# Hybrid decoder trunk in fp32: the low-rank rows and the rotary key are turned through HBM scratch and VectorE instead of TensorE, small projections three units later, last output piece 128 wide

## The chip, the cores and the metric

The kernel runs on one core of a Trainium2 chip. TensorE (PE) multiplies, VectorE (DVE) and ScalarE (ACT) compute element by element, GpSimd (POOL) does small things, SyncE (SP) issues nearly all transfers between HBM and the on-chip memory. The metric is the device time of the program in microseconds (us), as a median of several runs.

## The reference

The input is x, 256 tokens of width 1024, in float32. Two layers follow, and a final RMSNorm. One layer is a mixer of three branches with gates, and a squared-ReLU MLP:

```python
h = rms_norm(x, attn_norm[l])
p = h @ w_in
(cq, ckv, k_rope, mq, mk, mv, rq, rk, rv, rg, g_mla, g_moba, g_ret) = jnp.split(p, IN_SPLIT_IDX, axis=-1)
...
cq = rms_norm(cq, q_norm_g)            # 256 columns
ckv = rms_norm(ckv, kv_norm_g)         # 128 columns
q = (cq @ w_q_up)                      # 8 heads of 64 + 32 (rotary)
kv = (ckv @ w_kv_up)                   # 8 heads of 64 + 64
k_pe = apply_rope(k_rope, cos, sin)    # one rotary key of 32 columns for all heads
...
merged = (jax.nn.sigmoid(g_mla) * (o_mla @ w_branch_mla)
          + jax.nn.sigmoid(g_moba) * (o_moba @ w_branch_moba)
          + jax.nn.sigmoid(g_ret) * (o_ret @ w_branch_ret))
x = x + merged @ w_out
x = x + jnp.square(jax.nn.relu(rms_norm(x, mlp_norm[l]) @ w_up)) @ w_down
```

The change bears on cq, ckv and k_rope: after the projection they lie with tokens across the partitions ("rows"), and the next products want them with tokens along the free dimension, so they are turned.

## The kernel before

The 256 tokens are two tiles of 128 (t = 0, 1). Weights are streamed once, in the order that `weight_plan` writes down, as tiles `raw` of 128x1024 (four buffers). ScalarE rounds each to its high part `whi` and VectorE forms the remainder `wlo` (L211, L213, six buffers each). Each product of the reference is made of three on TensorE, high by high, high by low, low by high (`three`, L232 to L234), which share an accumulator in PSUM.

The work of a layer is a list of units (`prog`), each some twelve products on one weight tile: `start` (layer 0) or `b0` and `mq`, then `mk`, `mv`, the gates `gmla0`, `gmla1`, `gmoba0`, `rqk`, `rv`, `gmoba1`, `rg`, the branches `bmla0` and so on, `wout`, then the MLP. `at(slot(key, j), step)` hangs other work behind unit j of a key: attention scores, turns, group norm. A scheduler then settles each engine's own order from this program order. So what stands at which slot decides how much product work lies between a step and its user.

Two ways of turning a matrix are in use. One is a TensorE transpose into PSUM. The other is a round trip: `send` (L391) writes a 128x1024 tile `far` to HBM scratch with one transfer of 512 KB, `receive` (L397) reads it back as `blocks` with four transfers of 128 KB that put 32x32 blocks in their places, and `turn_into` (L405) transposes within the blocks on VectorE. SP issues all these transfers, in one line with the weights.

`c_norms` (from L571) copies the first projection to `c0`, scales cq and ckv by their norms and writes the turned rotary key `krx`. `c_turn` (L657) transposes these by eight TensorE instructions (six at L666, two at L669) into PSUM tiles `pct`, splits them with the gain into `cTh` and `cTl` (L247 on ScalarE, L248 on VectorE), and copies the rotary part through `krT` into the keys `KK` (L674 to L676). The small projections `qrope`, `qnope` and `kvup` use cTh and cTl; they are inserted before units mv0, mv1 and mv2, and the scheduler lets their products mix with those of mv. The attention steps are counted from `first`, which is the slot of unit mv3.

The end of the program is written out by hand. The last output half (columns 512 to 1023 of tile t = 1) is made in two pieces of 256 columns, by 12 products each. After the first piece VectorE adds (L1135), and multiplies by the final gain (L1171); after the last piece (`plast`) it adds (L1137), sums the squares (L1175), forms the sum `fst` (L1178). GpSimd raises it to the power -1/2 (L1183), ScalarE scales one half (L1184) and VectorE the other, and two transfers write the output.

Of the kernel before, what the change touches and what calls it, by code (L numbers as in the profile page):

```python
# [13 lines left out]
P = 128  # L14
# [44 lines left out]
def weight_plan():  # L59
# [20 lines left out]
    for l in range(L):  # L80
# [11 lines left out]
        mv, plan = plan[-4:], plan[:-4]  # L92
        for i, (key, name, kt, cols) in enumerate(
            (("qrope", "mla_w_q_up", 2, C_QROPE), ("qnope", "mla_w_q_up", 2, C_QNOPE), ("kvup", "mla_w_kv_up", 1, C_KV))
        ):
            block((l, key), name, kt, cols, kt)
            plan.append(mv[i])
        plan.append(mv[3])
        for i in range(2):
            gate("mla", i)  # L100
# [46 lines left out]
def trunk(ctx: ExitStack, tc: tile.TileContext, gx, wts, consts, gfin, gnorm, xtok, out):  # L147
# [28 lines left out]

    krx = [cp.tile([P, P], F32, name=f"krx{t}") for t in range(NT)]
    for t in range(NT):
        nc.gpsimd.memset(krx[t], 0.0)
# [56 lines left out]
    def gain(c):  # L236
        return G[:, c : c + 1]
# [326 lines left out]
    def layer(l, xn, before):  # L564

        c0 = []
# [4 lines left out]
        def c_norms():  # L571
            accs = b0
            if l:
                for n in range(KD):
                    xn.square(n)
                xn.stats()
            for t in range(NT):
                ct = w2k("c0")
                c0.append(ct)
# [8 lines left out]
                nc.vector.tensor_scalar(ct[:, 0:MLA_QR], ct[:, 0:MLA_QR], m[:, 4:5], None, op0=ALU.mult)  # L588
                kv = ct[:, MLA_QR : MLA_QR + MLA_KVR]
                nc.vector.tensor_scalar(kv, kv, m[:, 5:6], None, op0=ALU.mult)  # L590
                kr = ct[:, 384:416].rearrange("p (h two n) -> p h two n", h=1, two=2)
                rope(kr, K_COS_MLA, K_SIN_MLA, t, 16, 1, 32)
                for i in range(2):
                    dst = krx[t][:, 64 * (1 - i) : 64 * (1 - i) + 64].rearrange("p (two n) -> p two n", two=2)
                    nc.vector.tensor_copy(dst[:, :, 16 * i : 16 * i + 16], kr[:, 0, :, :])
# [61 lines left out]
        def c_turn():  # L657
# [4 lines left out]
            pts = [misc_tile("pct") for _ in range(2)]  # L662
            for k in range(3):
                pt = pts[k // 2][:, (k % 2) * S : (k % 2) * S + S]
                for t in range(NT):
                    nc.tensor.transpose(pt[:, P * t : P * t + P], c0[t][:, P * k : P * k + P], ident)  # L666
            pkr = pts[1][:, S : 2 * S]
            for t in range(NT):
                nc.tensor.transpose(pkr[:, P * t : P * t + P], krx[t], ident)  # L669
            for k in range(3):  # L670
                pt = pts[k // 2][:, (k % 2) * S : (k % 2) * S + S]
                split(pt, c["h"][:, k, :], c["l"][:, k, :], gain(G_CQ + 3 * l + k))
            krT = sb.tile([P, S], F32, name="krT", tag="xsq", bufs=2)
            nc.scalar.activation(krT, pkr, AF.Copy)  # L674
# [3 lines left out]
        at(slot("mk", 1 if l else 2), c_turn)  # L678
# [103 lines left out]
        at(first + 26, lambda: omobaT.extend((t4("omobah"), t4("omobal"))))  # L782
# [33 lines left out]
        attention(omobaT, moba_score, lambda: mqkv["mv"], MB_D**-0.5, [first + i for i in (11, 14, 17, 20)], first + 28)  # L816
# [3 lines left out]
        or_ps, aT, gn, oret = [], {}, [], []  # L820
# [36 lines left out]
        def group_norm():  # L857
# [23 lines left out]
            oret.append(both)  # L881
# [8 lines left out]
        def rg_done(accs):  # L890
            for t in range(NT):
                z, th, o = w2k("rg"), w2k("tg"), oret[0][:, :, t]
# [3 lines left out]
                nc.vector.scalar_tensor_tensor(o, o, 0.5, z.rearrange("p (g w) -> p g w", g=4), op0=ALU.mult, op1=ALU.mult)  # L896
            oret[0] = send(oret[0])
# [395 lines left out]
```

## Time and profile before

| | before |
|---|---|
| median of 3 runs | 815.45 us (815.39 to 815.56) |
| the profiled execution, device time | 814.98 us |
| its span in the profile | 812.9 us |
| PE busy | 804.9 us (99%), 3860 instructions |
| VectorE busy | 586.8 us (72%) |
| ScalarE busy | 458.3 us (56%) |
| GpSimd busy | 29.2 us (4%) |
| chain of work that ended last | PE 97% |
| mean DMA rate | 237 GB/s |

Busy time is the union of an engine's instructions; a short product's own duration in a timeline overlaps the next one's, so the step from start to start says what one costs. The chain is followed back from the last instruction to what released it.

### The profile page before, as it was taken

Reading aid. Unit: us, or ns where it says so; the run is one execution under the profiler, and the core shown is the slowest. Engines: PE = TensorE matmul, PEld = TensorE weight load, DVE = VectorE, ACT = ScalarE, POOL = GpSimd, SP = SyncE. Lnnn points to the kernel's source line nnn. Section 1 sums busy time; section 2 is a strip of 40 time slices with the busy share of each in tenths; the row PEclk is TensorE's granted clock in tenths of the full one; section 3 lists DMA queues with packets and bytes.
Section 4 is the critical chain, followed back from the end, with each engine's and each line's share of the span. In section 5 each row is a group of like instructions: output and inputs, shape, how many; then the busy total and the mean of one; then the engine's idle time right before and its main releaser. Section 6 shows DMA issues by size and latency. Waiting matters only on the chain.

```text
span 812.9 us, 11108 instructions
## 1 busy us (share of the span) xinstructions
PE 804.9 (99%) x3860; PEld 668.7 (82%) x3860; DVE 586.8 (72%) x1062; ACT 458.3 (56%) x714; POOL 29.2 (4%) x37
## 2 busy tenths in 40 slices
PE   9999999999999999999999999999999999999996
PEld 7888778888888888888888887788888888888885
DVE  6877897877786566666589678878778767665655
ACT  7686655555565455454577856646455555454542
POOL 0100000000040000000000000000002200000000
PEclk9999999999999999999999999999999999999999
DMA  9886989677567777777468778885675788887851
GB/s 352 293 299 195 281 267 264 191 226 231 176 212 249 221 257 259 253 239 243 152 207 249 247 236 252 298 258 182 206 236 178 238 268 273 281 273 246 258 184 52
DMA packets 75799, 192.72 MB, mean 237 GB/s; under 512 B 8416, under 2 KB 32352, under 8 KB 75744
## 3 DMA queue, kind: packets, MB, share of 16 engines
q1 hardware_dynamic: 75168, 191.16, 72.8%
q10 hardware_dynamic: 576, 0.87, 0.3%
q8 instruction: 30, 0.49, 0.2%
q14 instruction: 25, 0.20, 0.1%
HBM read 169.97 MB, written 22.02 MB: 236 GB/s over the span
## 4 chain that ended last, share of the span: by engine, by line
PE 97%; DMA 1%; issue 1%; DVE 0%; ACT 0%; SPq 0%; POOLq 0%; POOL 0%; DVEq 0%
PE acc L232 21%; PE acc L233 21%; PE acc L234 21%; PE pup L234 7%; PE pup L233 7%; PE pup L232 7%; PE acc L971 4%; PE acc L973 2%; PE po L470 1%; PE ps_s L746 1%; PE ps_s L441 1%; DMA raw<-wts 1%; PE ps_s L745 0%; PE acc L637 0%; PE acc L636 0%
## 5 line engine op out<-in xcount | busy, mean ns | idle before, releaser
L211 ACT ACTIVATE whi<-raw 128x1024 fp32r<-128x1024 f32 (+3 forms) x286 | 291.3, 1026 | 223.3 <-PE acc L234 125.2
L213 DVE TENSOR_TENSOR wlo<-raw,whi 128x1024 fp32r<-128x1024 f32 (+3 forms) x286 | 335.0, 1179 | 105.8 <-ACT whi L211 104.9
L232 PE MATMUL acc<-whi,xs 128*128 128x512 f32 (+1 forms) x384 | 151.8, 396 | 0.0
L234 PE MATMUL acc<-whi,xs 128*128 128x512 f32 (+1 forms) x384 | 149.3, 390 | 0.0
L233 PE MATMUL acc<-wlo,xs 128*128 128x512 f32 (+1 forms) x384 | 149.2, 389 | 0.0
L234 PE MATMUL pup<-whi,xs 128*128 128x512 f32 x256 | 99.8, 390 | 0.0
L233 PE MATMUL pup<-wlo,xs 128*128 128x512 f32 x256 | 99.6, 389 | 0.0
L232 PE MATMUL acc<-whi,hidden 128*128 128x512 f32 (+1 forms) x256 | 99.4, 388 | 0.0
L232 PE MATMUL pup<-whi,xs 128*128 128x512 f32 x256 | 99.3, 389 | 0.0
L233 PE MATMUL acc<-wlo,hidden 128*128 128x512 f32 (+1 forms) x256 | 99.2, 387 | 0.0
L234 PE MATMUL acc<-whi,hidden 128*128 128x512 f32 (+1 forms) x256 | 98.6, 388 | 0.0
L232 PEld LDWEIGHTS acc<-whi,xs 128*128 128x128 f32 x384 | 72.0, 188 | 16.6 <-issue 1.0
L234 PEld LDWEIGHTS acc<-whi,xs 128*128 128x128 f32 x384 | 72.1, 188 | 14.6
L233 PEld LDWEIGHTS acc<-wlo,xs 128*128 128x128 f32 x384 | 72.2, 188 | 13.8
L406 DVE STREAM_TRANSPOSE turnedup<-blocks 128x512 f32<-128x512 f32 x32 | 22.6, 708 | 55.0 <-DMA blocks<-far 55.0
L233 PEld LDWEIGHTS pup<-wlo,xs 128*128 128x128 f32 x256 | 48.0, 188 | 9.9
L234 PEld LDWEIGHTS acc<-whi,hidden 128*128 128x128 f32 x256 | 48.1, 188 | 9.8
L233 PEld LDWEIGHTS acc<-wlo,hidden 128*128 128x128 f32 x256 | 48.1, 188 | 9.8
L232 PEld LDWEIGHTS acc<-whi,hidden 128*128 128x128 f32 x256 | 48.0, 188 | 9.8
L234 PEld LDWEIGHTS pup<-whi,xs 128*128 128x128 f32 x256 | 48.1, 188 | 9.7
L232 PEld LDWEIGHTS pup<-whi,xs 128*128 128x128 f32 x256 | 48.0, 188 | 9.8
L251 ACT ACTIVATE hidden<-turnedup 128x512 fp32r<-128x512 f32 x32 | 20.3, 633 | 58.6 <-DVE turnedup L406 58.6
(234 smaller groups left out, 957.1 us busy)
## 6 DMA issues: line engine op xcount, KB each, us to landing
raw<-wts SPq DMA_DIRECT2D x264, 512.0 KB, 4.5
blocks<-far SPq DMA_DIRECT2D x104, 128.0 KB, 3.0
far<-relu SPq DMA_DIRECT2D x16, 512.0 KB, 3.8
far<-blocks SPq DMA_DIRECT2D x16, 384.0 KB, 4.2
turned<-far SPq DMA_DIRECT2D x64, 96.0 KB, 3.3
raw<-wts SPq DMA_DIRECT2D x7, 464.0 KB, 8.0
raw<-wts SPq DMA_DIRECT2D x4, 416.0 KB, 4.8
xrow<-xtok SPq DMA_DIRECT2D x4, 256.0 KB, 7.9
```

Of the source, the lines that this page charges most:

```text
L211: nc.scalar.activation(hi[:, cs], raw[:, cs], AF.Copy)
L213: nc.vector.tensor_sub(lo[:, cs], raw[:, cs], hi[:, cs].bitcast(F32))
L232: nc.tensor.matmul(o, ah, bh, start=start, stop=False)
L233: nc.tensor.matmul(o, ah, bl, start=False, stop=False)
L234: nc.tensor.matmul(o, al, bh, start=False, stop=stop)
L251: nc.scalar.activation(hi, src, AF.Copy)
L406: nc.vector.transpose(dst.rearrange("p n (a c) -> p n a c", a=4), src)
L441: nc.tensor.matmul(o, a[rows], b[rows], start=True, stop=True)
L470: nc.tensor.matmul(dst, vh, moving, start=i == 0, stop=i == 1)
L746: nc.tensor.matmul(o[:, P : 3 * P], q[:, P:S], k, start=True, stop=True)
L971: nc.tensor.matmul(acc, w[0][:, k, :], m, start=k == 0, stop=False)
L973: nc.tensor.matmul(acc[:, :S], w[1][:, k, :], mT[k // 4][:, k % 4, 0], start=False, stop=k == KD - 1)
```

## The change

- The rows and the rotary key of both tiles are written into one tile `crows` of the form that `send` takes (L587 and L595 of the kernel after), and sent at the end of `c_norms`. `receive` stands at unit mk1 in layer 0 and mq3 in layer 1. `c_turn` stands at mv0 in layer 0 and mk2 in layer 1 and does two VectorE transposes into `cturned`. The split and the key copies read from there. The 16 TensorE transposes and ScalarE's copies to krT are gone.
- `qrope` is inserted before mv3, `qnope` before gmla0 0, `kvup` before gmla0 1; the weights are in that order too. `first` is gmla0 2, three units later.
- MoBA's score pairs are at `first` + 11, 13, 16, 19 (were 11, 14, 17, 20) and its values at bmla0 1 (was `first` + 28). The retention turn, scores and values stand at gmoba1 2, rg 1 and rg 3 (were gmoba1 0, gmoba1 3 and rg 1). The multiplication by the gate rg is done in `group_norm`, which sends the result itself.
- The last output piece begins at column CUT = 896, so the two pieces are 384 and 128 wide.

```diff
+        for i in range(2):
+            gate("mla", i)
+        mv, gmla, plan = plan[-12:-8], plan[-8:], plan[:-12]
+        plan += mv[:3]
+        for (key, name, kt, cols), behind in (
+            (("qrope", "mla_w_q_up", 2, C_QROPE), mv[3:]),
+            (("qnope", "mla_w_q_up", 2, C_QNOPE), gmla[:1]),
+            (("kvup", "mla_w_kv_up", 1, C_KV), gmla[1:]),
         ):
             block((l, key), name, kt, cols, kt)
-            plan.append(mv[i])
-        plan.append(mv[3])
+            plan += behind
...
+            rows = pair_tile("crows")
+            nc.gpsimd.memset(rows[:, :, :, 96:], 0.0)
...
-                nc.vector.tensor_scalar(ct[:, 0:MLA_QR], ct[:, 0:MLA_QR], m[:, 4:5], None, op0=ALU.mult)
-                kv = ct[:, MLA_QR : MLA_QR + MLA_KVR]
-                nc.vector.tensor_scalar(kv, kv, m[:, 5:6], None, op0=ALU.mult)
+                for k in range(3):
+                    nc.vector.tensor_scalar(
+                        rows[:, :, t, 32 * k : 32 * k + 32], ct[:, P * k : P * k + P].rearrange("p (g c) -> p g c", g=4),
+                        m[:, 4 + k // 2 : 5 + k // 2], None, op0=ALU.mult,
+                    )
...
+                    c0 = 96 + 16 * i
+                    nc.vector.tensor_copy(rows[:, 2 * (1 - i) : 4 - 2 * i, t, c0 : c0 + 16], kr[:, 0, :, :])
+            c["far"] = send(rows)
...
-            pts = [misc_tile("pct") for _ in range(2)]
+            turned = sb.tile([P, 4, S], F32, name="cturned", tag="t4", bufs=T4)
+            for t in range(NT):
+                turn_into(turned.rearrange("p n (t c) -> p n t c", t=NT)[:, :, t], c["in"][t])
             for k in range(3):
-                pt = pts[k // 2][:, (k % 2) * S : (k % 2) * S + S]
-                for t in range(NT):
-                    nc.tensor.transpose(pt[:, P * t : P * t + P], c0[t][:, P * k : P * k + P], ident)
...
+                split(turned[:, k], c["h"][:, k, :], c["l"][:, k, :], gain(G_CQ + 3 * l + k))
+            krT = turned[:, 3]
             nc.vector.tensor_copy(KK[0:64, 1::2, :], krT[0:64, None, :].to_broadcast([64, 4, S]))
             nc.vector.tensor_copy(KK[64:P, 0::2, :], krT[64:P, None, :].to_broadcast([64, 4, S]))
 
-        at(slot("mk", 1 if l else 2), c_turn)
+        def c_in():
+            c["in"] = receive(c["far"])
+
+        at(slot(*(("mq", 3) if l else ("mk", 1))), c_in)
...
-        for i, unit in enumerate((qrope, qnope, kvup)):
-            prog.insert(slot("mv", i), ((unit.__name__, 0), unit))
-        at(slot("mv", 1), qr_turn)
+        at(slot(*(("mk", 2) if l else ("mv", 0))), c_turn)
...
+        for unit, behind in ((qrope, ("mv", 3)), (qnope, ("gmla0", 0)), (kvup, ("gmla0", 1))):
+            prog.insert(slot(*behind), ((unit.__name__, 0), unit))
+        at(slot("gmla0", 0), qr_turn)
...
-        first = slot("mv", 3)
+        first = slot("gmla0", 2)
...
-        attention(omobaT, moba_score, lambda: mqkv["mv"], MB_D**-0.5, [first + i for i in (11, 14, 17, 20)], first + 28)
+        attention(omobaT, moba_score, lambda: mqkv["mv"], MB_D**-0.5, [first + i for i in (11, 13, 16, 19)], slot("bmla0", 1))
...
-            oret.append(both)
+                o = both[:, :, t]
+                nc.vector.scalar_tensor_tensor(o, o, 0.5, rg[t].rearrange("p (g w) -> p g w", g=4), op0=ALU.mult, op1=ALU.mult)
+            oret.append(send(both))
...
-        at(slot("gmoba1", 0), ret_turn)
+        at(slot("gmoba1", 2), ret_turn)
         for i in range(2):
-            at(slot("gmoba1", 3), lambda i=i: ret_scores(i))
+            at(slot("rg", 1), lambda i=i: ret_scores(i))
         for h in range(RT_H):
-            at(slot("rg", 1), lambda h=h: ret_values(h))
-        at(slot("rg", 1), group_norm)
+            at(slot("rg", 3), lambda h=h: ret_values(h))
+        at(slot("rg", 3), group_norm)
...
-                    cs = slice(512 + 256 * half, 768 + 256 * half)
+                    cs = slice(CUT, D) if half else slice(512, CUT)
+                    n = cs.stop - cs.start
...
+CUT = 896
```

How the order on the engines changes is shown at the place in layer 0 where the turned rows are made and used. Lines of the kernel after are two lower from L196 on, so L230 to L232 there are the three products. On PE before, the transposes of c and krx stand among the products of mv (xs is the normed input, whi and wlo a weight tile):

```order
L234 MATMUL acc<-whi,xs_91 128x512
L666 MATMUL pct<-K,c_339 128x128 x2
L666 MATMUL pct<-K,c_358 128x128
L666 MATMUL pct<-K,c_339 128x128
L666 MATMUL pct<-K,c_358 128x128 x2
L669 MATMUL pct<-K,krx_81 128x128
L232 MATMUL acc<-whi,xs_91 128x512
```

On PE after, at the first use of the turned rows in layer 0 (qrope into misc, qnope into acc):

```order
L232 MATMUL acc<-whi,xs_90 128x512
L230 MATMUL misc<-whi,cTh 128x256
L231 MATMUL misc<-wlo,cTh 128x256
L230 MATMUL misc<-whi,cTh 128x256
L231 MATMUL misc<-wlo,cTh 128x256
L230 MATMUL acc<-cTh,whi 128x256 x2
L232 MATMUL misc<-whi,cTl 128x256
```

The transposes are gone, all 48 products of mk and all 48 of mv now stand ahead of the first product with cTh, and six products with cTh stand ahead of the first with cTl.

On VectorE before, the key copies of layer 0, with the splits cTl and rotations of mk around them:

```order
L248 SCALAR_TENSOR_TENSOR cTl<-pct,GX,cTh 128x256 x2
L366 TENSOR_TENSOR mk<-ropea,ropeb 128x4x8
L367 TENSOR_TENSOR mk<-ropea,ropeb 128x4x8
L213 TENSOR_TENSOR wlo<-raw,whi 128x1024
L364 TENSOR_TENSOR ropea<-mk,K 128x64
L365 TENSOR_TENSOR ropeb<-mk,K 128x64
L675 COPY KK<-krT 64x4x256
L676 COPY KK<-krT 64x4x256
```

On VectorE after, the same place:

```order
L211 TENSOR_TENSOR wlo<-raw,whi 128x1024
L404 STREAM_TRANSPOSE cturned<-blocks 128x4x128 x2
L211 TENSOR_TENSOR wlo<-raw,whi 128x1024
L669 COPY KK<-cturned 64x4x256
L670 COPY KK<-cturned 64x4x256
L246 SCALAR_TENSOR_TENSOR cTl<-cturned,GX,cTh 128x256 x3
L211 TENSOR_TENSOR wlo<-raw,whi 128x1024
```

The three splits cTl, which stood ahead of the key copies, now stand behind the transposes, one weight split and both key copies. On SP after, the transfers of this stretch of layer 0:

```order
L194 DMA raw<-wts 128x1024 x5
L392 DMA far<-crows 128x1024
L392 DMA far<-mq 128x1024
L194 DMA raw<-wts 128x1024
L399 DMA blocks<-far 32x4x256 x8
L392 DMA far<-mk 128x1024
```

The rows' send is new and stands ahead of mq's; their four receives are among the eight behind one weight load, where before four stood.

## Rows read from the trace of the kernel before

**Rows 1.** Busy time by stretches: stretch, us, engines' busy us, PE clock, DMA.

```profile
0.00:8.00 8.00, 6.36 (x21) 4.76 (x21) 2.56 (x6) 4.18 (x8) 0.76 (x9) 1.00 0.76 264
8.00:806.50 798.50, 798.49 (x3840) 663.98 (x3840) 582.44 (x1051) 453.43 (x706) 27.86 (x27) 1.00 0.74 238
```

**Rows 2.** Timeline of PE, layer 1: start us, us, operation, count [idle before].

```profile
433.27 0.38 PE L666 MATMUL pct<-K,c 128*128 128x128 f32 x2
...
433.72 0.60 PE L666 MATMUL pct<-K,c 128*128 128x128 f32 x4
434.15 0.38 PE L669 MATMUL pct<-K,krx 128*128 128x128 f32 x2
...
434.61 0.39 PE L234 MATMUL acc<-whi,xs 128*128 128x512 f32 x1
...
438.94 0.28 PE L232 MATMUL misc<-whi,cTh 128*128 128x256 f32 x1
```

**Rows 3.** Timeline of PE, first and last of the 24 end products.

```profile
803.51 0.28 PE L232 MATMUL acc<-whi,hidden 128*128 128x256 f32 x1
...
806.26 0.28 PE L234 MATMUL plast<-whi,hidden 128*128 128x256 f32 x1
```

**Rows 4.** Timeline of VectorE, the tail.

```profile
805.87 0.42 DVE L1171 TENSOR_TENSOR y<-xr,gf 128x256 f32<-128x256 f32 x1
806.58 0.42 DVE L1137 TENSOR_TENSOR xr<-xr,plast 128x256 f32<-128x256 f32 x1 [0.29 <-PE plast L234]
...
807.57 0.22 DVE L1178 SCALAR_TENSOR_TENSOR fst<-fst 128x1 f32<-128x1 f32 x1
```

**Rows 5.** Timeline of ScalarE, the tail.

```profile
808.46 0.72 ACT L1184 ACTIVATE y<-y,fr 128x512 f32<-128x512 f32 x1 [2.08 <-POOL fr L1183]
```

**Rows 6.** Timeline of VectorE, layer 0, around the rows and their turn.

```profile
35.35 0.28 DVE L590 TENSOR_SCALAR c<-c,ssc 128x128 f32<-128x128 f32 x1
...
36.22 1.22 DVE L213 TENSOR_TENSOR wlo<-raw,whi 128x1024 fp32r<-128x1024 f32 x1
...
37.64 0.27 DVE L595 COPY krx<-c 128x32 f32<-128x32 f32 x2
...
39.85 0.48 DVE L248 SCALAR_TENSOR_TENSOR cTl<-pct,GX,cTh 128x256 fp32r<-128x256 f32 x1 [0.78 <-ACT cTh L247]
...
46.45 0.69 DVE L676 COPY KK<-krT 64x1024 f32<-64x1024 f32 x1
...
55.56 1.30 DVE L406 STREAM_TRANSPOSE turnedqk<-blocks 128x512 f32<-128x512 f32 x2
```

**Rows 7.** Timeline of PE, layer 0, first product of mk.

```profile
25.65 0.39 PE L232 MATMUL acc<-whi,xs 128*128 128x512 f32 x1
```

**Rows 8.** Timelines of SP and VectorE: sends, receives and first transposes of round trips.

```profile
155.69 0.33 SPq L394 DMA_DIRECT2D far<-oret  x1
165.54 0.45 DVE L406 STREAM_TRANSPOSE oy<-blocks 128x256 f32<-128x256 f32 x1 [2.03 <-DMA blocks<-far]
435.91 0.42 SPq L394 DMA_DIRECT2D far<-mq  x1
442.72 1.75 SPq L401 DMA_DIRECT2D blocks<-far  x4
645.39 0.33 SPq L394 DMA_DIRECT2D far<-relu  x1
653.11 0.71 DVE L406 STREAM_TRANSPOSE turnedup<-blocks 128x512 f32<-128x512 f32 x1 [2.07 <-DMA blocks<-far]
```

**Rows 9.** Timelines of PE and VectorE, layer 0: retention's last products, low part, use.

```profile
143.51 0.39 PE L855 MATMUL por<-rv,prob 128*128 128x128 f32 x2
168.59 1.28 DVE L252 TENSOR_TENSOR oretl<-oy,oreth 128x512 fp32r<-128x512 f32 x2
179.39 0.39 PE L232 MATMUL acc<-whi,oreth 128*128 128x512 f32 x1
```

**Rows 10.** Timeline of PE, the first products of the program.

```profile
1.42 3.51 PE L546 MATMUL warm<-zero 128*128 128x512 f32 x8 [1.42 <-DVE zero L175]
```

More of the change, by code (lines that the diff above doesn't have):

```diff
@@ L91, in weight_plan @@
         block((l, "mv"), "w_in", KD, C_MV, 2)
-        mv, plan = plan[-4:], plan[:-4]
-        for i, (key, name, kt, cols) in enumerate(
-            (("qrope", "mla_w_q_up", 2, C_QROPE), ("qnope", "mla_w_q_up", 2, C_QNOPE), ("kvup", "mla_w_kv_up", 1, C_KV))
+        for i in range(2):
[6 more added lines that the diff above has]
+            (("kvup", "mla_w_kv_up", 1, C_KV), gmla[1:]),
         ):
             block((l, key), name, kt, cols, kt)
-            plan.append(mv[i])
-        plan.append(mv[3])
-        for i in range(2):
-            gate("mla", i)
+            plan += behind
         gate("moba", 0)
@@ L175, in trunk @@
     nc.vector.tensor_copy(zero, zf)
-    krx = [cp.tile([P, P], F32, name=f"krx{t}") for t in range(NT)]
-    for t in range(NT):
-        nc.gpsimd.memset(krx[t], 0.0)
     order, loaded = list(where), {}
@@ L661, in c_turn @@
             mla["v"] = [w2k("vml") for _ in range(NT)]
-            pts = [misc_tile("pct") for _ in range(2)]
+            turned = sb.tile([P, 4, S], F32, name="cturned", tag="t4", bufs=T4)
+            for t in range(NT):
+                turn_into(turned.rearrange("p n (t c) -> p n t c", t=NT)[:, :, t], c["in"][t])
             for k in range(3):
-                pt = pts[k // 2][:, (k % 2) * S : (k % 2) * S + S]
-                for t in range(NT):
-                    nc.tensor.transpose(pt[:, P * t : P * t + P], c0[t][:, P * k : P * k + P], ident)
[L667 to L674, printed above, removed]
+                split(turned[:, k], c["h"][:, k, :], c["l"][:, k, :], gain(G_CQ + 3 * l + k))
+            krT = turned[:, 3]
             nc.vector.tensor_copy(KK[0:64, 1::2, :], krT[0:64, None, :].to_broadcast([64, 4, S]))
             nc.vector.tensor_copy(KK[64:P, 0::2, :], krT[64:P, None, :].to_broadcast([64, 4, S]))
-        at(slot("mk", 1 if l else 2), c_turn)
+        def c_in():
+            c["in"] = receive(c["far"])
+        at(slot(*(("mq", 3) if l else ("mk", 1))), c_in)
         def nope(dst, w, ks, copy):
@@ L781, in layer @@
             branch(l, "bmla", half, omlaT, th_mla, merged)
-        at(first + 26, lambda: omobaT.extend((t4("omobah"), t4("omobal"))))
+        at(slot("bmla0", 0), lambda: omobaT.extend((t4("omobah"), t4("omobal"))))
         qkT = {}
@@ L895, in rg_done @@
                 nc.vector.scalar_tensor_tensor(z, th, 1.0, z, op0=ALU.add, op1=ALU.mult)
-                nc.vector.scalar_tensor_tensor(o, o, 0.5, z.rearrange("p (g w) -> p g w", g=4), op0=ALU.mult, op1=ALU.mult)
-            oret[0] = send(oret[0])
+                rg.append(z)
         def oret_in():
@@ L1172, in layer @@
                     else:
-                        add(t, cs, more[:, 0:256])
+                        add(t, cs, more[:, 0:n])
                         junk = w2k("fsq")
                         nc.vector.tensor_tensor_reduce(
-                            junk[:, 0:256], xr[:, t, cs], xr[:, t, cs], 1.0 / D, EPS, ALU.mult, ALU.add, st[:, 5:6]
+                            junk[:, 0:n], xr[:, t, cs], xr[:, t, cs], 1.0 / D, EPS, ALU.mult, ALU.add, st[:, 5:6]
                         )
```

12 lines of the change are left out of this document (4 added, 8 removed).

## The prediction

> **What bounds the kernel now.** I read the busy time by stretches first: TensorE (PE) works 798.49 of the 798.50 us between 8 and 806.5 us [rows 1]. So only three things can move the time: work taken from PE, work given to PE, and a new moment at which PE waits. VectorE, ScalarE and the DMA queues cost nothing until they are late for PE or carry the tail. After that I read the timeline of each place that the diff touches: the TensorE transposes, the last products and the tail behind them, and the stretch of layer 0 in which the low-rank rows are used. A product of 512 columns comes every 0.228 us (19 steps from 434.61 to 438.94) [rows 2], one of 256 columns every 0.1196 us (23 steps from 803.51 to 806.26) [rows 3].
>
> **Transposes taken away.** In layer 1 the eight transposes stand between 433.27 and 434.61, with two 512-wide products among them [rows 2]: 1.34 - 2 x 0.228 = 0.884 us. Layer 0 has eight of the same shape, so PE loses 2 x 0.884 = **-1.77 us**. On the other side each layer gains one send of 512 KB, four receives of 128 KB, two VectorE transposes and two scalings; VectorE and the queue have room for them on average, and what they cost depends on when their result is there (below).
>
> **Tail, last piece 128 wide.** The last 24 products took 23 steps of 0.1196, so 2.87 us with the last. Now 12 are 384 wide, which I put halfway between the two rates, 0.174, so 2.09 us; 12 are 128 wide. No product of this kind and width is in the trace. A line through the rates of 512 and 256 goes to 0.066 at 128, and a product of 128 columns should not be dearer than one of 512, 0.228: these are the ends. The nearest row is the TensorE transpose of 128 columns, four in 0.43 from 433.72 to 434.15 [rows 2], 0.108 each. I take 0.11: 1.32 us. PE then ends 2.09 + 1.32 - 2.87 = +0.54 later (ends: +0.01 and +1.96).
>
> VectorE behind it: the multiply for the first piece started at 805.87, the last addition at 806.58, 0.32 after PE's last start [rows 3, 4]. The first piece is now ready (2.09 - 12 x 0.1196 = 0.65) later, so the multiply starts at 806.52 and, 384 wide, is done at 807.08: VectorE took 0.42 for 256 columns [rows 4] and 0.28 for a 128-wide scaling [rows 6], so I put 384 at 0.56. PE's last start at 806.80 frees the last addition at 807.12. Its 128 columns take 0.28 instead of 0.42, and the reduction behind it saves the same, so the sum of squares, formed at 807.57 before, comes at 807.57 + 0.54 - 0.28 = 807.83: **+0.26**. After it ScalarE's 512-wide scaling of 0.72 [rows 5] is not changed, so VectorE's two steps beside it, of which one gets narrower and one wider, gain nothing. The ends of the 128-wide step give +0.22 (then the 384-wide multiply sets it: 807.08 for 806.58, less 0.28) to +1.7.
>
> **Layer 0, the new wait.** Before, the small projections could start as soon as eight transposes and the split were done. Now their operands go rows, HBM, receive, VectorE transposes, split, and PE meets them after the 96 products of mk and mv. PE's side: the first mk product starts at 25.65 [rows 7]; 96 x 0.228 = 21.9; PE arrives at 47.5. Six 256-wide products use only the high part (cTh), 0.72; at 48.25 it needs the low part (cTl).
>
> The operand's side: VectorE's last write of the rotary key began at 37.64 and took 0.27 [rows 6], so it ends at 37.9. Six scalings for four add some 0.4, and one weight split ahead of them is now only 512 wide, which takes about 0.55 off; I leave 37.9. How long the round trip takes I read from the kernel's other ones, from the send's issue to VectorE's first transpose: retention output 155.69 to 165.54 = 9.85; the quickest 645.39 to 653.11 = 7.7; the slowest was sent at 435.91 and its receives were issued only at 442.72 [rows 8], 6.8 later; with half of 9.85 for the way back, an estimate of 11.7. I take 9.85, since here too a send of 512 KB and weight loads share the queue: transposes start at 47.75. Two of 512 columns took 1.30 [rows 6]: 49.05. Then VectorE's order has one weight split (1.22, so about 1.15 to the next start), two copies into KK (0.69 each) and the first cTl (0.48) [rows 6]: 50.2, 51.6, 52.1. PE waits from 48.25 to 52.1: **+3.9 us**. Nothing fills it: the products behind it in PE's order all need cTh or cTl, and the next gate unit stands behind them. Others queue behind the waits: on SP the send of the rows holds mq's send and the weight load behind it until 37.9; on VectorE the transposes, and on ScalarE the high part cTh, hold the next weight splits. All these weights are for products behind the projections, and PE has the weights of mv and of all three projections by then, so I add nothing. With the quickest trip the wait is 3.9 - 2.15 = 1.75; with 11.7 it is 5.75.
>
> The Trainium skill, page "DMA: Bandwidth & Descriptors", section "Anatomy of one DMA — SWDGE (gpsimd) path", gives a transfer as 2.0 us plus its bytes / 436 KB per us; for the way out and back that is an estimate of 3.2 + 3.2 = 6.4 us, and the wait would be about 0.45. The trace disagrees: even its quickest trip takes 7.7, and the sum goes by 9.85.
>
> **Layer 1.** PE comes to the projections 96 products after the start of mk, which is 0.88 earlier than 438.94 + 48 x 0.228 = 449.9, so 449.0, and needs cTl at 449.7. The transposes on PE started at 433.27, when the rows were ready; with the send I put the full rows at about 434.6 (an estimate: the added scalings and a few rope steps behind it). 434.6 + 9.85 + 1.30 + two copies 1.38 + a split 1.15 + 0.48 = 448.8. So **0**, with 0.9 to spare; a trip of 11.7 gives +0.95.
>
> **Moved steps.** The retention values and norm, the MoBA values, and the pairs' scores issue the same instructions as before, only at other units; PE's share stays. What could be late is the retention output for its branch: from the last products (143.51) to its low part done (168.59 + 1.28) it took 26.4, and PE used it at 179.39 [rows 9], 35.9 after them. The products are now 24 steps (one unit, 5.5 us) later, which leaves 30.4: covered by 4. MoBA's output is now used 24 products after its values, 5.5 us, where the order of before had 48; the group norm that stood in VectorE's way there lost the gate's multiplies to an earlier place. I count both at **0**.
>
> **Sum**, on the profiled execution: 814.98 - 1.77 + 0.26 + 3.9 + 0 = 817.4; that execution lies 0.47 below the median, so **817.8** as the median. A difference under 0.2% (1.6 us: 813.8 to 817.1) is about what a measurement here cannot tell from none. Without any wait the sum is 813.9.
>
> **Rivals.**
> - *The wait is short.* A trip of 7.7 gives a wait of 1.75 and 815.7; each step of VectorE that goes ahead of the transposes, up to the split and the copies, takes its time off as well. For it: the two sides are only 4 us apart in a sum of six terms. Against it: the retention output's trip, of the same size and in the same layer, took 9.85 [rows 8]. By the page's figure above the time would be 814.4.
> - *No wait and a good tail: faster.* It needs the operand by 48.25, so 3.9 off the chain, and the tail at its low end: 813.5 to 813.8. Mechanism: the rows are sent two us earlier and the trip is the quickest; it decides at a wait below 0. The trace of before shows no such pair.
> - *Half rate after the wait.* The first eight 512-wide products of the program took 3.51 [rows 10], 0.44 each. If PE comes back so from a wait of 3.9, eight products cost another 1.7: 819.5. Against it: the granted clock reads 1.00 over that first stretch [rows 1], and the wait is short.
> - *A late hand-off later*, retention or MoBA output, by 2 us in each layer: 821.8. It decides when the retention chain takes over 30.4 or MoBA's over 5.5.
> - *128-wide products at 0.228*: tail +1.7 instead of +0.26: 819.3.
>
> **Chances.** The forecast (a layer-0 wait from 3.2 to 5.6, 817.1 to 819.5) 0.44; wait short 0.33; faster 0.12; the three that add to the wait together 0.11. Slower is 0.44 + 0.11 = 0.55, within 0.2% 0.33, faster 0.12. The range, 813.9 to 820.8, leaves out the faster case and about half of the last three; the forecast's own range is 817.1 to 819.5.
>
> **What would show it.** Right: no transposes on PE before the projections, one gap on PE of 3 to 5 us near 48 to 52 released by VectorE's cTl, none near 449, last product about 0.5 later after the tail's start. Wrong: no gap in layer 0 (then the trip or the rows were earlier than I read), a gap in layer 1, gaps at the retention or MoBA branch, or 128-wide steps far from 0.11.

## The result and the profile after

The changed kernel takes **824.86 us** (median of six runs, 821.61 to 826.58) where the kernel before takes 815.42 (814.64 to 816.02) on the same chip: a ratio of 1.0110, interval 1.0088 to 1.0131. It is slower, as was the likeliest case, but by 9.4 us and not by 2.4, and the time lies outside the range of 813.9 to 820.8. The profiled execution took 824.47 with a span of 822.2, 9.5 more than that of before.

Where TensorE (PE) waited is read from its view of waits. Columns: who waited for whom, us in total, how often, the longest.

```profile
PE misc L230 <- ACT cTh L245: 3.5, 1, 3.5
...
PE ps_r L439 <- DVE turnedrqk L404: 1.2, 1, 1.2
PE por L852 <- DVE prob L845: 1.2, 1, 1.2
PE misc L232 <- DVE cTl L246: 0.9, 2, 0.7
```

Before, PE was busy for 798.49 of 798.50 us after its start [rows 1]; now four waits stand there. The first is the forecast one, at the turned rows; the last is the rest of it, with 0.2 in layer 1. The two between are new: the retention scores (ps_r) wait for their turned queries and keys, and the values (por) for prob, which VectorE makes from those scores.

The timeline of PE at the first wait (start, us, operation, idle before it):

```profile
47.06 0.39 PE L232 MATMUL acc<-whi,xs 128*128 128x512 f32 x1
50.91 0.58 PE L230 MATMUL misc<-whi,cTh 128*128 128x256 f32 x1 [3.46 <-ACT cTh L245]
51.29 0.42 PE L231 MATMUL misc<-wlo,cTh 128*128 128x256 f32 x1
...
53.30 0.58 PE L232 MATMUL misc<-whi,cTl 128*128 128x256 f32 x1 [0.73 <-DVE cTl L246]
53.68 0.41 PE L230 MATMUL misc<-whi,cTh 128*128 128x256 f32 x1
53.89 0.41 PE L231 MATMUL misc<-wlo,cTh 128*128 128x256 f32 x1
...
56.88 0.31 PE L230 MATMUL acc<-cTh,whi 128*128 128x256 f32 x1
57.02 0.28 PE L231 MATMUL acc<-cTl,whi 128*128 128x256 f32 x1
57.14 0.28 PE L232 MATMUL acc<-cTh,wlo 128*128 128x256 f32 x1
...
58.58 0.40 PE L230 MATMUL acc<-whi,xs 128*128 128x512 f32 x1
```

Two things are to be seen. PE was done with mv at 47.06 + 0.23 = 47.29 and could have used the low part six products later, at 48.0; it got it at 53.30, so the wait is **5.3 us**. And behind the wait a 256-wide product comes every 0.213 us (53.68 to 53.89) until about 56.9, and only then every 0.12 as in [rows 3]: 15 steps that cost 0.093 more each, **1.4 us**. The view by stretches shows the same as a clock (columns as in [rows 1]):

```profile
50.00:54.00 4.00, 2.35 (x9) 2.06 (x10) 3.96 (x8) 2.26 (x4) 0.00 (x0) 0.51 1.02 412
54.00:58.00 4.00, 4.00 (x25) 4.00 (x25) 2.25 (x6) 1.52 (x4) 0.00 (x0) 0.64 1.03 412
58.00:62.00 4.00, 4.00 (x22) 3.40 (x21) 3.18 (x7) 3.93 (x7) 0.00 (x0) 1.00 0.34 87
```

The granted clock is 0.51, the level of 1.2 GHz, right after the idle stretch, and 1.00 again from 58 on. The Trainium skill, page "TensorE: Matmul & The Clock Gate", section "Back-to-back issue gap", gives the step at the lower level as the columns over 1.2 GHz, by which 256 columns are an estimate of 213 ns; the trace agrees with 0.213 us.

The operand's side, from the timelines of VectorE, SP and ScalarE:

```profile
36.69 1.23 DVE L211 TENSOR_TENSOR wlo<-raw,whi 128x1024 fp32r<-128x1024 f32 x1
...
38.62 0.27 DVE L595 COPY crows<-c 128x32 f32<-128x32 f32 x2
...
49.02 1.30 DVE L404 STREAM_TRANSPOSE cturned<-blocks 128x512 f32<-128x512 f32 x2 [4.20 <-DMA blocks<-far]
50.24 1.18 DVE L211 TENSOR_TENSOR wlo<-raw,whi 128x1024 fp32r<-128x1024 f32 x1
51.35 0.68 DVE L669 COPY KK<-cturned 64x1024 f32<-64x1024 f32 x1
52.04 0.69 DVE L670 COPY KK<-cturned 64x1024 f32<-64x1024 f32 x1
52.76 1.27 DVE L246 SCALAR_TENSOR_TENSOR cTl<-cturned,GX,cTh 128x256 fp32r<-128x256 f32 x3
```

```profile
38.96 0.33 SPq L392 DMA_DIRECT2D far<-crows  x1
39.34 0.42 SPq L392 DMA_DIRECT2D far<-mq  x1
...
43.03 4.23 SPq L399 DMA_DIRECT2D blocks<-far  x8
```

The rows are ready at 38.9, are sent at 38.96, and VectorE's first transpose starts at 49.02, after 4.20 of its own idle time: a round trip of 10.06. The order of the steps behind it is the forecast one.

The transposes on PE are gone. At the end of the program PE's 128-wide products follow one another at 0.11 us (the last three start at 815.63, 815.74 and 815.86), and its last product starts 9.60 later than before [rows 3].

### The profile page after: what moved, and what is told of

It reads as the page before. It is cut to its first block, busy times and chain, and to the rows that moved or that the text cites. A ratio compares the mean times of both kernels' runs of the same rounds, so it can differ in the third digit from the quotient of the medians.

```text
span 822.2 us, 11085 instructions
## 1 busy us (share of the span) xinstructions
PE 807.9 (98%) x3844; PEld 670.4 (82%) x3844; DVE 587.5 (71%) x1070; ACT 455.9 (55%) x712; POOL 29.4 (4%) x37
## 4 chain that ended last, share of the span: by engine, by line
PE 79%; DVE 8%; DMA 6%; issue 3%; ACT 2%; SPq 1%; POOL 0%; POOLq 0%; DVEq 0%; ACTq 0%
PE acc L230 16%; PE acc L231 16%; PE acc L232 16%; PE pup L232 7%; PE pup L231 7%; PE pup L230 7%; PE acc L970 4%; DVE wlo L211 3%; DMA blocks<-far 2%; DMA raw<-wts 2%; PE acc L972 2%; PE po L468 1%; DMA far<-crows 1%; ACT whi L209 1%; DMA far<-blocks 1%
## 5 line engine op out<-in xcount | busy, mean ns | idle before, releaser
L230 PE MATMUL acc<-whi,xs 128*128 128x512 f32 (+1 forms) x384 | 151.5, 395 | 0.0
L232 PE MATMUL acc<-whi,xs 128*128 128x512 f32 (+1 forms) x384 | 148.8, 389 | 0.0
L232 PE MATMUL pup<-whi,xs 128*128 128x512 f32 x256 | 99.8, 390 | 0.0
L230 PE MATMUL acc<-whi,hidden 128*128 128x512 f32 (+1 forms) x256 | 99.6, 389 | 0.0
L230 PE MATMUL pup<-whi,xs 128*128 128x512 f32 x256 | 99.3, 389 | 0.0
L232 PE MATMUL acc<-whi,hidden 128*128 128x512 f32 (+1 forms) x256 | 98.8, 388 | 0.0
L230 PEld LDWEIGHTS acc<-whi,xs 128*128 128x128 f32 x384 | 72.0, 188 | 17.1 <-issue 2.0
L232 PEld LDWEIGHTS acc<-whi,xs 128*128 128x128 f32 x384 | 72.1, 188 | 14.8
L231 PEld LDWEIGHTS acc<-wlo,hidden 128*128 128x128 f32 x256 | 48.1, 188 | 9.9
L230 PEld LDWEIGHTS acc<-whi,hidden 128*128 128x128 f32 x256 | 48.1, 188 | 9.9
L232 PEld LDWEIGHTS pup<-whi,xs 128*128 128x128 f32 x256 | 48.1, 188 | 9.6
L232 PEld LDWEIGHTS acc<-whi,hidden 128*128 128x128 f32 x256 | 48.0, 188 | 9.7
L230 PEld LDWEIGHTS pup<-whi,xs 128*128 128x128 f32 x256 | 47.9, 188 | 9.8
```

Source lines behind the costliest of these rows:

```text
L230: nc.tensor.matmul(o, ah, bh, start=start, stop=False)
L231: nc.tensor.matmul(o, ah, bl, start=False, stop=False)
L232: nc.tensor.matmul(o, al, bh, start=False, stop=stop)
```

## The experiments

Their medians are compared with the kernel before on the same chip; edits are to the changed kernel where nothing else is said.

### Which part loses the time

**The order of after, with the TensorE transposes.** Both layers make the turned rows as before; the later projections, the moved steps and the cut at 896 stay.

```diff
+                    nc.tensor.transpose(pt[:, P * t : P * t + P], c0[t][:, P * k : P * k + P], ident)
...
-        at(slot(*(("mk", 2) if l else ("mv", 0))), c_turn)
+        at(slot("mk", 1 if l else 2), c_turn)
```

> The changed kernel, but the rows and the rotary key are turned by the eight TensorE transposes of before, at mk2 and mk1; the three-unit delay of the small projections, the moved attention and retention steps and the 384/128 tail stay. Theory A (the loss begins at the wait for the turned rows in layer 0): no gap of PE near 47 to 57 us and no half clock there; of the changed kernel's excess the 6.5 us that this stretch lost come back and 1.8 us of transposes return, so about 820. Theory B (the wait for the retention rows near 145 us and for prob near 154 us is a follow-up of the layer-0 wait): these two gaps (2.7 us) go too, so about 817. If they stay, the moved steps make them by themselves. Rival C (the three-unit delay and the moved steps cost the time, not the turn): about 824, as the changed kernel.

815.97 for 815.27, ratio 1.0007 (0.9998 to 1.0016). PE waits only at the program's start. So the moved steps, the later projections and the new cut cost some 0.7 us at most by themselves, and neither the first wait nor those at the retention appear without the turn through HBM.

**The cut alone**, on the kernel before.

```diff
-                    cs = slice(512 + 256 * half, 768 + 256 * half)
+                    cs = slice(CUT, D) if half else slice(512, CUT)
...
+CUT = 896
```

> The kernel before with only the last output piece changed to 384 and 128 columns. My sum: PE ends 0.5 later and the program 0.26 later, so 815.7, ratio 1.0003, nothing that can be told from none. If 128-wide products cost no less than their columns' share, the program ends 0.2 later; if as much as a 512-wide one, 1.7 later. Rival: the shorter last piece shortens the tail by more than PE loses, ratio below 0.9995.

815.55 for 815.27, 1.0014 (1.0000 to 1.0028): too small for the medians, so the timelines of PE and VectorE decide.

```profile
806.67 0.28 PE L233 MATMUL plast<-wlo,hidden 128*128 128x128 f32 x1
806.79 0.28 PE L234 MATMUL plast<-whi,hidden 128*128 128x128 f32 x1
```

```profile
806.53 0.56 DVE L1172 TENSOR_TENSOR y<-xr,gf 128x384 f32<-128x384 f32 x1
807.10 0.29 DVE L1137 TENSOR_TENSOR xr<-xr,plast 128x128 f32<-128x128 f32 x1
...
807.83 0.22 DVE L1179 SCALAR_TENSOR_TENSOR fst<-fst 128x1 f32<-128x1 f32 x1
```

PE's last product starts at 806.79 (forecast 806.80), the sum of squares is formed at 807.83 (forecast 807.83), where it was 807.57 [rows 4]: +0.26.

**The HBM turn in one layer only.** The other layer keeps the TensorE transposes, in the order of after.

```diff
+        if FAR[l]:
...
+            at(slot(*(("mq", 3) if l else ("mk", 1))), c_in)
+        else:
...
+            at(slot("mk", 1 if l else 2), c_turn)
...
+FAR = (False, True)
```

> The changed kernel with the turn through HBM and VectorE in layer 1 only; layer 0 turns by the TensorE transposes as before (at mk2). Theory A (layer 0 makes the loss; layer 1 hides the trip but for 0.7 to 0.9 us of waits and gives back 0.88): like the run with TensorE turns in both layers, 815.9 to 816.2. Rival (layer 1 costs its share too, since the same queues are loaded): 817 or more.

In layer 1 only: 815.93 for 815.04, 1.0012 (1.0003 to 1.0022). PE waits 0.2 for cTl in the trace, and 1.2 for prob, both in layer 1.

> The changed kernel with the turn through HBM and VectorE in layer 0 only; layer 1 by the TensorE transposes. Theory A: the whole loss, 822 to 825, as the changed kernel. Rival (loss spread over both layers): 819 to 820.

In layer 0 only (FAR = (True, False)): 824.62, 1.0114 (1.0097 to 1.0131), as much as the whole change loses. It is made up otherwise, though. PE waits 4.6 for cTh and 0.7 for cTl and gets the low part 6.4 us after it could have used it (54.51 for 48.1), the half rate behind that costs 2.3 (25 steps), and at the retention PE waits only 0.3. The clock is low until about 60:

```profile
50.00:54.00 4.00, 1.65 (x6) 1.35 (x6) 3.73 (x6) 2.26 (x4) 0.00 (x0) 0.51 1.03 370
54.00:58.00 4.00, 3.49 (x16) 3.49 (x17) 2.38 (x4) 0.31 (x2) 0.00 (x0) 0.50 0.88 359
```

**No trip through HBM.** VectorE transposes the blocks of the rows where they lie, so that the turned rows are another matrix; PE does the products of after with it.

```diff
-            c["far"] = send(rows)
+            c["rows"] = rows
...
-                turn_into(turned.rearrange("p n (t c) -> p n t c", t=NT)[:, :, t], c["in"][t])
+                turn_into(turned.rearrange("p n (t c) -> p n t c", t=NT)[:, :, t], c["rows"][:, :, t].rearrange("p g (a c) -> p g a c", c=32))
```

> The changed kernel, with the rows of both layers turned on VectorE straight from the tile in which they are made, without send and receive (the 32x32 blocks stay in their places, so the turned rows are another matrix). The whole change but for the trip. Theory A (the trip is the whole loss): no gap near 47 us, none at the retention scores, and the 1.77 us of transposes are won against the run with TensorE turns: 815.97 - 1.77 = 814.2. Rival C (a part of the loss comes from VectorE's transposes or the moved steps): above 815.5.

814.64 for 815.12, 0.9988 (0.9978 to 0.9998); PE waits only at the start. VectorE's transposes, the key copies and the splits behind them still stand in its order, so it is the trip that loses the time. The gain is 0.5, though, where 1.5 was expected. The trace says why: PE's first mk product starts at 26.15 for 25.65 [rows 7], 0.5 later; from there to the first product of the MoBA branch it saves 0.71, from that to the same place in layer 1 0.67 (instead of 0.88 each), and the tail's 0.54 on PE comes on top: its last product starts 0.35 earlier in all.

### Half rate behind the wait

**Spare work on PE.** 22 products of 512 columns, whose result nobody reads, stand ahead of mv's last unit in layer 0, so that PE is busy while the rows are under way.

```diff
+            if l == 0:
+                spare = misc_tile("spare")
+                for i in range(FILL):
+                    nc.tensor.matmul(spare, wh[:, 0, 0:P], wh, start=True, stop=True)
...
+FILL = 22
```

> The changed kernel with 22 products of 512 columns into a spare PSUM tile ahead of the last unit of mv in layer 0, from the weights of the rope projection alone; the result is not touched. They take about 5.0 us of PE in the time in which it waits. Theory A (the half clock from 50.9 to 56.9 us comes from PE's idle time before it): the granted clock stays at 1.00, the 256-wide products step by 0.12 us instead of 0.21, and PE gains about 1.3 us (33 products behind the first with cTl at 53.3 end near 57.3 instead of 58.6). Rival (the clock falls for another reason, for instance DMA traffic): clock 0.5 there as before, no gain. In both the wait for the data itself stays, covered by the added products.

821.96 for 815.27, 1.0080 (1.0067 to 1.0093).

```profile
44.45 5.15 PE L696 MATMUL spare<-whi 128*128 128x512 f32 x22
...
53.64 0.39 PE L232 MATMUL misc<-whi,cTl 128*128 128x256 f32 x1 [0.60 <-DVE cTl L246]
53.86 0.28 PE L230 MATMUL misc<-whi,cTh 128*128 128x256 f32 x1
53.98 0.28 PE L231 MATMUL misc<-wlo,cTh 128*128 128x256 f32 x1
```

The operand comes at the same time, 53.6 for 53.3, and a kernel that does 5.0 us more on PE is no slower than the changed kernel: PE had that time to spare. Behind the wait the products now come every 0.12 and the granted clock stays at 1.00. The size of this effect alone was measured with the pairs of before, since the retention waits (below) also changed here:

> The run with MoBA's pairs as before (no retention gaps), with the 22 products into a spare tile in the layer-0 wait. Theory A (the half clock behind the idle time is a cost of its own): clock 1.00 at 50 to 58 us and about 1.3 us less than the run with the pairs alone, so 819.6 beside 820.9. Rival (the first fill gained only because the retention gaps were missing in it, and the half clock costs nothing, since cTl and the weights set the pace there): no difference between the two.

> The run with MoBA's pairs as before, unaltered, on the same chip as the run above, for the comparison: 820.9, the half clock at 50 to 57 us, no retention gaps.

On one chip, with the score pairs of before in both (the edit is shown under the waits at the retention): 821.26 with the 22 products (six runs, 819.26 to 822.59; 1.0063, interval 1.0040 to 1.0085), 822.42 without (six, 821.10 to 822.99; 1.0073, 1.0049 to 1.0097). The traces differ as expected (clock 1.00 with, 0.50 between 54 and 58 without). The medians differ by 1.2, near the 1.4 that the steps give, but the runs overlap: the time is not clear of their spread. Nor do the two traces differ in the clock alone: without the products the rows came 1.1 later (first transpose at 49.85 for 48.73), and with them PE has new waits of 0.8 for ScalarE. So the 1.4 rests on the steps, not on these medians.

### More distance does not help here

**Projections two units later in layer 0**, so that PE comes to the first product with cTh some 7 us later (54.4 for 47.3).

```diff
+        both, far = mv + gmla, 3 + LATER[l]
+        plan += both[:far]
...
+        for i, unit in enumerate((qrope, qnope, kvup)):
+            prog.insert(slot(*both[far + i]), ((unit.__name__, 0), unit))
...
+LATER = (2, 0)
```

> The changed kernel, with the small projections of layer 0 and the slot that its attention steps count from two units later still (qrope ahead of gmla0 1, qnope ahead of gmla0 2, kvup ahead of gmla0 3), so 5.4 us more of products ahead of the first with cTh; layer 1 as in the changed kernel. Theory A (the distance is too short by 5.2 us in layer 0): the gap near 47 us and the half clock vanish, 6.5 us come back: about 818.4. With theory B (the retention gaps follow from it) another 2.7: about 815.7. Rival (the wait moves along, since the scheduler or the queue holds the rows back too): a gap remains at the first cTh product, over 822.

823.82 for 815.27, 1.0107 (1.0092 to 1.0121): no better than the change itself. The first wait fell to 0.3 + 0.7. It did not vanish because the rows came later too: sent at 40.32, they were turned from 52.92 on, a trip of 12.60. And another wait came. PE and ScalarE:

```profile
71.15 0.50 PE L231 MATMUL acc<-whi,xs 128*128 128x512 f32 x1 [3.23 <-ACT KK L689]
```

```profile
66.39 1.06 ACT L210 ACTIVATE whi<-raw 128x1024 fp32r<-128x1024 f32 x1 [3.40 <-DMA raw<-wts]
```

ScalarE waits 3.4 for weights, everything behind it on ScalarE comes late, and PE waits for the last of it; the clock is 0.61 behind that wait as well (72 to 76). The DMA engines' busy share reads 1.01 from 64 to 68. My "I add nothing" for the weights queued behind the turn held only because PE was waiting for the rows anyway.

**The rows' transfers issued by GpSimd**, on the kernel with the two units, so that SP's weight loads aren't queued behind them.

```diff
-            c["far"] = send(rows)
+            c["far"] = send(rows, nc.sync if l else nc.gpsimd)
...
-            c["in"] = receive(c["far"])
+            c["in"] = receive(c["far"], queue=nc.sync if l else nc.gpsimd)
```

> The run with the projections of layer 0 two units later, with one more edit: in layer 0 the send of the rows and its four receives are issued by GpSimd, so that SP's line goes on with the weights. In that run the gap at the first cTh product was down to 1.1 us, but PE waited 3.4 us at 68 us, as ScalarE had waited for weight tiles (3.4 us) and SP had stood 5 us at the receives. Theory D (what waits in line behind the round trip, on SP and on VectorE, is the second cost): that gap goes and the time comes to 816 to 818. Rival 1 (the weight loads are late because the transfers themselves are at their limit): the gap stays, 822 to 824. Rival 2 (a transfer issued by GpSimd takes longer): the gap at the first cTh product returns.

825.67 for 815.04, 1.0131 (1.0116 to 1.0146), and the theory fell.

```profile
40.74 0.74 POOL L393 DMA_DIRECT2D far<-crows  x1 [4.41 <-DVE mk L366]
48.77 2.20 POOL L400 DMA_DIRECT2D blocks<-far  x4 [7.29 <-DMA far<-crows]
```

Sent at 40.74, the rows can be read only at 48.77, and VectorE's first transpose starts at 60.03: 19.3 us. PE waits 3.5 + 1.6 for the rows, now at 62 to 64, and ScalarE still waits 3.0 to 4.8 for weights. Taking the rows' transfers out of SP's line did not help; the DMA engines' share is 1.00 to 1.08 from 46 to 62.

**MoBA's queries without their trip in layer 0**, which stands right behind the rows' send.

```diff
-            qkT[key] = send(mqkv.pop(key))
+            qkT[key] = mqkv.pop(key) if (l, key) == (0, "mq") else send(mqkv.pop(key))
```

> The changed kernel, with MoBA's query of layer 0 turned on VectorE without its trip through HBM (its blocks are left in their places, so the query is another matrix); 1 MB of transfers beside the rows' trip falls away. Theory E (the rows' trip is long because the query's send and receives share the queues with it): the trip of the rows falls from 10 to about 8 us, the gap near 47 us from 3.5 to about 1.5, and with the shorter idle time the half clock may be gone: about 820. Rival (each trip takes its 10 us by itself): gap 3 us or more, time as the changed kernel, 822 to 825.

822.98 for 815.12, 1.0083 (1.0061 to 1.0105). The rows' trip took 9.76 for 10.06, though the DMA engines' share over it fell from 1.03 to 0.79, and PE still waits 3.2 + 1.6. That transfer is not what makes the trip long.

### The waits at the retention

**MoBA's score pairs at the units of before**: 11, 14, 17, 20 instead of 11, 13, 16, 19.

```diff
-        attention(omobaT, moba_score, lambda: mqkv["mv"], MB_D**-0.5, [first + i for i in (11, 13, 16, 19)], slot("bmla0", 1))
+        attention(omobaT, moba_score, lambda: mqkv["mv"], MB_D**-0.5, [first + i for i in (11, 14, 17, 20)], slot("bmla0", 1))
```

> The changed kernel, with MoBA's score pairs at 11, 14, 17 and 20 units behind the first slot, as before. Theory F (the pairs that stand closer crowd VectorE, so that the retention rows are sent late and PE waits at their scores and at prob): these gaps go (1.0 to 2.7 us in the two traces), 822 at most, the gap near 47 us unchanged. Rival (they are a follow-up of the layer-0 wait alone, as the run with TensorE turns has the same pairs and no such gap): the gaps stay or come and go as before, 822 to 826.

820.93 for 815.12, 1.0068 (1.0049 to 1.0086). The wait at the rows is there as in after (3.1 + 0.7), those at the retention are gone. VectorE's busy time (third of the busy columns) between 118 and 138, first in after, then in this kernel:

```profile
118.00:128.00 10.00, 10.00 (x68) 7.31 (x67) 10.00 (x32) 6.89 (x15) 0.00 (x0) 1.00 0.84 246
128.00:138.00 10.00, 10.00 (x48) 7.82 (x49) 9.96 (x30) 5.69 (x13) 0.00 (x0) 1.00 0.79 228
```

```profile
118.00:128.00 10.00, 10.00 (x69) 7.55 (x68) 9.97 (x31) 6.35 (x15) 0.00 (x0) 1.00 0.93 295
128.00:138.00 10.00, 10.00 (x49) 7.81 (x48) 8.00 (x23) 5.68 (x14) 0.00 (x0) 1.00 0.97 279
```

In after VectorE is full for 20 us on end. The retention's queries and keys are among its work there, and their send shows the delay:

```profile
134.61 0.43 SPq L392 DMA_DIRECT2D far<-rqk  x1
...
145.53 1.42 DVE L404 STREAM_TRANSPOSE turnedrqk<-blocks 128x256 f32<-128x256 f32 x4 [5.75 <-DMA blocks<-far]
...
146.78 1.58 PE L439 MATMUL ps_r<-turnedrqk 64*128 64x256 f32 x16 [1.25 <-DVE turnedrqk L404]
...
155.67 0.49 PE L852 MATMUL por<-rv,prob 128*128 128x128 f32 x2 [1.18 <-DVE prob L845]
```

With the pairs of before that send is issued at 128.67, 5.9 earlier. In the first experiment, with the closer pairs but no wait at the rows, it is issued at 124.69, the turn is done 3.5 us ahead of PE, and nothing waits. So the waits come only where the closer pairs meet the HBM turn, and not always there: with the projections two units later PE waits for neither. How late the rows are doesn't settle it: in the kernel with the HBM turn in layer 1 only, prob was waited for 1.2 in that layer behind a wait of 0.2 for the rows.

The traces show where VectorE lost time before that in layer 0 of after: it stood still for 6 us until the blocks of MoBA's key were there, whose receives SP issued only at 79.92.

```profile
90.48 1.42 DVE L404 STREAM_TRANSPOSE turnedqk<-blocks 128x256 f32<-128x256 f32 x4 [5.96 <-DMA blocks<-far]
```

```profile
55.20 24.67 SPq L194 DMA_DIRECT2D raw<-wts  x9
79.92 1.96 SPq L399 DMA_DIRECT2D blocks<-far  x4
```

In the order of after with TensorE's transposes in both layers, or without the trip, VectorE does not wait there; nor does it with the projections two units later. The more of this idle time a trace with the closer pairs has, the longer PE waits at the retention of layer 0, roughly: 5.96 and 2.75 in after, 4.29 and 1.0 in its second trace (below), 4.65 and 0.5 with the HBM turn in layer 0 only, 2.93 and none with the spare work. With the pairs of before it stands 4.73 (3.21 in the kernel before), and PE waits for nothing at the retention. This is a reading of traces and not shown: no run changed it alone, the run with GpSimd's transfers (PE waits 1.3 there) has no such stand at MoBA's key, and in layer 1 of the second trace VectorE stands 4.61 and PE waits for nothing at the retention. The waits also vary:

> The changed kernel once more, unaltered, for a second trace. Its runs lie between 821.6 and 826.6, far wider than those of the kernel before. Theory A (the layer-0 wait is always there, the retention gaps near 145 and 154 us are what comes and goes): the gap near 47 us is again 3 to 4 us with the half clock behind it, and if this run is near 822 the retention gaps are missing. Rival: the first gap itself varies by several us and the retention gaps are the same.

The unchanged kernel after, once more on another chip: 822.40 in its one run. The first wait is 3.2 + 0.7; at the retention only prob is waited for, 0.8. Between these two traces 1.8 us (2.75 for 1.0, with the restart) of the 2.1 by which their times differ lie at this place. It is not all that varies: in the two traces of the kernel with the pairs of before, where nothing waits at the retention, the trip took 10.29 and 11.24, PE got the low part at 52.89 and 54.13, and their times differ by 1.7 (820.76 and 822.48). What the runs' spread (821.6 to 826.6) is made of is not shown.

### A mix of the parts

**TensorE transposes in layer 0, the HBM turn in layer 1 one unit later, the cut at 768.**

```diff
+LATER = (0, 1)
+FAR = (False, True)
-CUT = 896
+CUT = 768
```

> What the runs so far point to: TensorE transposes in layer 0, the trip through HBM in layer 1 alone with its projections one unit later still, last pieces 256 wide as before. Against the run with the trip in layer 1 alone (815.93): 0.3 less for the tail, and the 0.7 us of waits for cTh and cTl in layer 1 covered: 814.9, ratio to the kernel before about 0.9998. Rival: the later unit meets the same shortage of weight tiles as in layer 0, over 816.

815.16 for 815.12, 0.9993 (0.9984 to 1.0002), and PE waits nowhere but at the start. It cannot be told from the kernel before.

## Why the prediction was wrong

Three steps failed: "Moved steps ... I count both at 0", which cost 2.75; the half rate behind the wait, left out of the sum, 1.4; and the moment at which the rows are sent, 1.06 of the 1.4 that the wait was too small. The terms, in us, for the profiled execution (9.5 longer than that of before):

```
term                                forecast  found   from
transposes, both layers              -1.77    -1.4    the run without the trip, 0.71 + 0.67
tail                                 +0.26    +0.26   the cut alone
layer 0, wait for the rows           +3.9     +5.3    timeline of PE, 48.0 to 53.30
layer 0, half rate behind it          0       +1.4    15 steps of 0.213 for 0.12
retention, scores and values          0       +2.75   starts of PE's products 1.41 and 1.34 later than their step
layer 1, wait for the rows            0       +0.7    timeline of PE, 458.65 to 459.32
start of the first mk product         0       -0.2    25.48 for 25.65
sum                                  +2.4     +8.8
```

Of the 0.7 us that this sum lacks, 0.26 lie in the first step behind the wait (53.30 to 53.68, 0.38 for 0.12); the rest is not placed.

- **The mechanism and its place: right.** One wait in layer 0, at the first products with the turned rows, with nothing on PE to fill it; the HBM turn in layer 0 alone loses as much as the whole change (in another mix: a longer wait and half rate, hardly any at the retention), and without the trip nothing is lost.
- **The size of that wait: 1.4 too small.** The trip was right, 10.06 for 9.85, with some luck: issued by SP in layer 0 it took 9.8 to 12.6 in the traces of the other runs, 10.40 in the second trace of the same kernel. The rows were sent at 38.96, 1.06 later than my 37.9: "I leave 37.9" took off 0.55 for a narrower weight split, but the split ahead of the rows is still 1024 wide and starts at 36.69 (36.22 before [rows 6]). PE came 0.25 earlier than I had it. The Trainium skill, page "DMA: Bandwidth & Descriptors", section "Anatomy of one DMA — SWDGE (gpsimd) path", gives a fixed 2.0 us and the bytes over a rate for a transfer issued by GpSimd, by which the trip was an estimate of 6.4; no trip of these rows was under 9.4 in any run, issued by SP or by GpSimd, and the measured one holds.
- **"Half rate after the wait" was no rival but part of the forecast.** I set it aside because the clock read 1.00 at the program's start and "the wait is short". The first did not speak against it: the eight products of [rows 10] came every 0.44, half the rate of 0.228, in a stretch whose clock reads 1.00. After 3.5 us of idle the clock read 0.51, and PE needed until 56.9 to be at full rate again. My 1.7 for it was near the 1.4 found; it belonged in the sum.
- **"Moved steps ... I count both at 0" failed.** I followed the retention's and MoBA's outputs to their branches, which were in time, as forecast, and did not follow the retention's input: queries and keys through VectorE, HBM and back to the scores, while the same diff puts MoBA's pairs closer together in VectorE's order. This is the largest single miss in the profiled execution, 2.75, and some 1 in the second one. In the traces VectorE loses up to 6 us beforehand, standing for MoBA's key; that this makes the waits, no run shows.
- **Weights behind the turn, "I add nothing": right at the projections of this kernel**, but only as long as PE waits for the rows; two units later they are the wait.
- **Layer 1: 0.7 for 0.** My spare time of 0.9 was used up by a trip of 11.5 (sent at 443.38, first transpose at 454.88) for 9.85; the bound of 11.7 had given 0.95.
- **Transposes and tail: right**, the tail to 0.02 at each of its steps; the transposes gave 0.7 a layer instead of 0.88.

All misses but that of the start have one sign: together they made the loss four times the forecast one.

## What to carry to other kernels

In a kernel that keeps TensorE busy throughout, a round trip is free only where enough other work stands in front of its first use, as in layer 1 of the mix: before a hand-off goes through HBM, compare its whole chain, from the last write of the source to the first use, with the work that stands between, and count a slower clock behind the gap as part of the gap. Where a change moves steps, follow each one's inputs as well as its outputs, on the engine that its new neighbours fill. More distance helps only if what is queued behind has time to spare too; here the weight stream did not.

## What the runs showed of the hardware that was not expected

- An idle stretch of 3.46 us put PE's granted clock from 1.00 to 0.51, and the products of the next 6 us came at half rate; after the gaps of 1.4 and 1.3 at 145 and 154 it read 1.00.
- In the kernel with the projections two units later, the same send and receives took 12.60 us issued by SP and 19.3 issued by GpSimd; the DMA engines' share over the trip was 0.81 and 0.98.
- A 128-wide product follows the one before it after 0.11 us, hardly less than a 256-wide one after 0.12: here, columns cut from 256 to 128 save PE next to nothing.
- The program's start is not the same from trace to trace: the first mk product started at 25.65 in before, 25.48 in after and 26.15 in the kernel without the trip, since PE's first 416-wide products came at half rate (0.35 for 0.19) for a different time. The granted clock of these stretches reads 1.00 all the same.
